# Modulation weights in runs of four row tiles, laid out by row tile

## The chip, the cores and the metric

The kernel runs on one core of one Trainium2 chip. The metric is the time of one execution on the device, in microseconds. The change was timed against the kernel before on the same chip; a profiled execution of each shows where the time goes. The core has five engines with a queue of instructions each: TensorE (PE: matmuls, PEld: its weight loads), VectorE (DVE), ScalarE (ACT), GpSimd (POOL) and SyncE (SP), which only issues transfers.

## The reference

The reference is one layer of a bidirectional encoder, applied to a prompt of 1024 tokens and a sample of 256, each with its own conditioning vector c. All is in float32 with a model width of 1024.

```python
mod = (jax.nn.silu(c) @ ada_w[l] + ada_b[l])[:, None, :]
sh1, sc1, g1, sh2, sc2, g2 = jnp.split(mod, 6, axis=-1)
h = rms_norm(x, norm_mix_g[l]) * (1 + sc1) + sh1
proj = h @ w_in[l]
...
x = x + g1 * ((g_na * y_na + g_mla * y_mla) @ w_out[l])
h2 = rms_norm(x, norm_ffn_g[l]) * (1 + sc2) + sh2
x = x + g2 * hierarchical_moe(h2, ...)
```

The modulation is a vector times a matrix of 1024 x 6144, for two vectors. Its first third (sh1, sc1) scales the input of the projections and is needed at once. The second (g1, sh2) and the third (sc2, g2) are needed only after the attention. The projection to 3,968 columns gives queries, keys and values of a neighbourhood attention, the latents of a second attention (with normalized latents and a rotary part), and the logits of the gates.

## The kernel before

The order of the work is written out by hand: each engine runs its instructions in the order of the program, and waits for other engines and for transfers by semaphores. What an operation waits for is worked out from the tiles that it reads and writes.

All large tiles are slots of one pool, 49 of 128 x 1024 floats (`Slots`, 4 KB in each partition). `get` takes the slot that has been free longest, `put` gives it back at once in program order. The next user of a slot then waits on its own engine until the last reader is through, and that can be a transfer that stores the slot to HBM.

The change lies in the stretch in which the input projections run, about 79 to 327 us of the span. The three chunks of tokens are 512, 512 and 256 wide. `work(g, ...)` does one group of 128 columns of w_in: its matmuls (line 432: each operand is split into a high and a low half, three products), then the split of the next group's weights (line 182 on ACT the high half, line 183 on DVE the low half), the load of the group after it, and the evacuation of PSUM. The groups are lat[1], qq (queries), kk (keys), gt (gates) and vv (values). The functions that `work` is given after the group run in between:

- `latent_stat` and `latent_norm` (PE line 519, DVE lines 522 and 524, ACT line 523) normalize the latents.
- `uq_part(n)` (PE line 557) projects the latents to queries. For n of 4 and 5 it is followed by `rope`, for each of the three chunks: DVE shuffles and scales (lines 536 to 538), POOL adds (line 539), then `split_out` splits the sum (ACT line 399, DVE line 400) and SP stores it (line 405, rq_d).
- `split_out` after the query and key groups does ACT line 402 or 399, DVE line 403 or 400, and stores at line 405 as well (naq_d, nak_d).
- `ukv_part` (PE line 570) and `vml_part` (PE line 584) come later.

Between all of these, `ada_step` does a little of the second and third modulation, so that it costs no stretch of its own. The weights of one row tile (128 rows of the 1024) for a half of a third of the modulation are 128 x 1024 numbers. POOL loads them (line 370); PE multiplies them in four matmuls of 32 weight columns and 256 moving columns, which stand side by side in the four quarters of the array (line 382, tile_position), and so sum up in PSUM over the eight row tiles. When a modulation is complete, DVE adds the bias (line 387) and SP stores it (line 389). There are 2 x 2 x 8 = 32 row tiles.

The order of the calls that the change moves along:

```python
work(gt[0], lambda: latent_norm(0))
work(qq[2], lambda: latent_norm(1, 2), lambda: lat_split("uq", uq_raw, 768))
work(qq[3], uq(4))
work(gt[1], uq(5))
uq_done()
work(gt[2], uq(0))
work(kk[0], uq(1))
```

Each `work` has one call of `ada_step` behind the group and one behind each function.

Of the kernel before, what the change touches and what calls it, by code (L numbers as in the profile page):

```python
# [33 lines left out]
def by_blocks(x):  # L34

    return np.ascontiguousarray(x.reshape(*x.shape[:-2], 16, 8, 8, x.shape[-1]).swapaxes(-4, -3)).reshape(x.shape)
# [54 lines left out]
def v3(t, k):  # L91
    return t.rearrange("p (k n) -> p k n", k=k)
# [3 lines left out]
def kernel(ctx, tc, A, out_p, out_s, upto=99, dbg=None):  # L96
    nc = tc.nc
    ctx.enter_context(tc.manual_schedule())
    V, S, G, PE, SY = nc.vector, nc.scalar, nc.gpsimd, nc.tensor, nc.sync
# [11 lines left out]
    def pool(name, bufs=1, space=None, stack=None):  # L111
        kw = dict(name=name, bufs=bufs, reuse_waits="tile")
        if space is not None:
            kw["space"] = space
        return (stack or ctx).enter_context(tc.tile_pool(**kw))
# [21 lines left out]
    sl = Slots(pool("slots"), NSLOT)  # L137
# [22 lines left out]
    ada_v = A["ada_w"].rearrange("o (p j) n -> (o p) j n", j=8)  # L160
# [54 lines left out]
    cT = small.tile([128, 8, 32], F32, name="cT")  # L215
# [9 lines left out]
    def bias_load(s):  # L225
        b = small.tile([128, 512], F32, name="biasz")
        G.memset(b, 0.0)
        for r in range(2):
            if s:
                SY.dma_start(b[r:128:32], A["ada_b"][:, s * 2048:(s + 1) * 2048].rearrange("o (g n) -> (o g) n", g=4))  # L230
            else:
                for v in range(2):
                    SY.dma_start(b[64 * v + r:64 * v + 64:32].rearrange("p (h n) -> p h n", h=2),
                                 A["ada_b"][:, v * 1024:(v + 1) * 1024].rearrange("o (h q n) -> (o q) h n", h=2, q=2))
        return b
# [94 lines left out]
    for j in range(KD):  # L330
# [7 lines left out]
        for n, (a, b) in enumerate(((0, hH), (1, hH), (0, hL))):  # L338
            for i in range(2):
                for c, (c0, w) in enumerate(CHUNKS):  # L340
                    PE.matmul(ps0[i][c][:, :w], order[0].at(a, j, i * 128, 128), b.at(j, c),  # L341
                              start=(j == 0 and n == 0 and (c < 2 or i == 0)), stop=(j == KD - 1 and n == 2),
                              skip_group_check=(c == 2))
    for j in range(KD):
        for c, (c0, w) in enumerate(CHUNKS):
            PE.matmul(pk[32 * c:32 * c + 32, :w], v3(kr, 8)[:, j, :32], xT.at(j, c), start=(j == 0), stop=(j == KD - 1),
                      tile_position=(0, 32 * c), skip_group_check=True)
# [11 lines left out]

    adas = [(s, hf, j) for s in (1, 2) for hf in range(2) for j in range(8)]
    ada_q = []
    ada_pm = {}

    def ada_pre():
        if adas:
            s, hf, j = adas.pop(0)
            t = sl.get()
            G.dma_start(v3(t, 4), ada_v[:, j, s * 2048:(s + 1) * 2048].rearrange("p (g n) -> p g n", g=4)[:, :, hf * 256:hf * 256 + 256])  # L370
            ada_q.append((s, hf, j, t))

    def ada_step():
        if not ada_q:
            return
        s, hf, j, t = ada_q.pop(0)
        if (hf, j) == (0, 0):
            ada_pm[s] = psm.tile([128, 512], F32, name="pm0" if s == 1 else "pmt")
            biasz[s] = bias_load(s)
        pm = ada_pm[s]  # L380
        for g in range(4):
            PE.matmul(pm[32 * g:32 * g + 32, hf * 256:hf * 256 + 256], cT[:, j, :], v3(t, 4)[:, g, :],
                      start=(j == 0), stop=(j == 7), tile_position=(0, 32 * g), skip_group_check=True)
        sl.put(t)
        if (hf, j) == (1, 7):
            row = small.tile([128, 512], F32, name="modrow")
            V.tensor_add(row, pm, biasz[s])
            for r in range(2):
                SY.dma_start(mod_d[s - 1, r].rearrange("(g n) -> g n", n=512), row[r:128:32, :])
        ada_pre()  # L390
# [17 lines left out]
    def work(g, *after):  # L408


        gi = order.index(g)
        def ahead():
            if gi + 1 < len(order):
                order[gi + 1].split()
            if gi + 2 < len(order):
                order[gi + 2].load()

        g.run(ahead)
        ada_step()
        for f in after:  # L420
            f()
            ada_step()
        g.put()
# [27 lines left out]
            sl.put(t)  # L451
        return f

    for _ in range(3):
        ada_pre()
    order[1].split()
    order[2].load()
# [544 lines left out]
            next(fill_it)  # L1002
        work(gt[i])
    while ada_q:
        ada_step()
    for x in (hH, hL):
        for c in (1, 2):
            x.put(c)
# [65 lines left out]
    n = len(units)  # L1074
# [388 lines left out]
    for c, (c0, w) in enumerate(CHUNKS):  # L1463
# [25 lines left out]
        if c == 1:  # L1489
# [3 lines left out]
            t = sl.get(ring=rows)  # L1493
# [211 lines left out]
def layout(inputs):  # L1705

    a = {k: np.ascontiguousarray(inputs[k]) for k in _INS}
    q = a["w_uq"].reshape(1, 256, 8, 96)
    a["w_uq"] = np.ascontiguousarray(np.concatenate(
        [q[..., :64].reshape(1, 256, 512), q[..., 64:].reshape(1, 256, 256)], axis=2))  # L1710
    kv = a["w_ukv"].reshape(1, 128, 8, 128)
    a["w_ukv"] = np.ascontiguousarray(np.concatenate(
        [kv[..., :64].reshape(1, 128, 512), kv[..., 64:].reshape(1, 128, 512)], axis=2))
    inv = (np.float32(1.0) / np.power(np.float32(10000.0), np.arange(0, 32, 2, dtype=np.float32) / np.float32(32)))
    ang = np.arange(SP, dtype=np.float32)[:, None] * inv[None, :].astype(np.float32)
    c, s = np.cos(ang).astype(np.float32).T, np.sin(ang).astype(np.float32).T
    cs = np.stack([np.tile(np.concatenate(x), (4, 1)) for x in ((c, c), (-s, s))])
    a["rope_p"] = by_blocks(cs[..., None])[..., 0]
    a["rope_s"] = np.ascontiguousarray(cs[:, :, :SS])
    a["x_prompt"] = by_blocks(a["x_prompt"])  # L1720

    rpb = a.pop("na_rpb")[0]
    row, c8, col = np.arange(16), np.arange(8), np.arange(64)
    rs = np.clip(row - 4, 0, 8)
    rows = (row[None, :] >= rs[:, None]) & (row[None, :] < rs[:, None] + 8)
    dr = np.clip(row[None, :] - row[:, None] + 7, 0, 14)
    dc = 8 * (np.arange(3)[None, :, None] - 1) + c8[None, None, :] - c8[:, None, None]
    val = rpb[:, dr[:, None, None, :, None], np.clip(dc + 15, 0, 30)[None, :, :, None, :]]  # L1730
    m0 = np.broadcast_to(rows[:, None, None, :, None], val.shape[1:]) & (np.abs(dc) < 16)[None, :, :, None, :]
    m1 = m0 & ((dc >= -8) & (dc < 8))[None, :, :, None, :]
    a["nbias"] = np.ascontiguousarray(np.stack(
        [np.where(m, val, np.float32(NEG)).reshape(8, 128, 384) for m in (m0, m1)], axis=2).reshape(8, 128, 768))
    st = np.clip(col - 8, 0, 48)
    inside = (col[None, :] >= st[:, None]) & (col[None, :] < st[:, None] + 16)
    dr = np.arange(6)[None, :] + 5 - np.arange(2)[:, None]
    dc = np.clip(col[None, :] - col[:, None] + 15, 0, 30)
    val = rpb[:, dr[:, None, :, None], dc[None, :, None, :]]
    a["sbias"] = np.ascontiguousarray(np.where(inside[None, None, :, None, :], val, np.float32(NEG)).reshape(8, 128, 384))  # L1740
    return a
# [18 lines left out]
```

## Time and profile before

| | |
|---|---|
| times of three runs | 1855.3, 1858.37, 1858.37 us (median 1858.37) |
| the profiled execution | 1854.83 us, of which the span of its instructions is 1853.1 |
| PE | 1743.1 us busy, 94% of the span |
| PE's weight loads | 1357.6 us, 73% |
| DVE, ACT, POOL | 1001.4, 838.8 and 319.0 us (54, 45 and 17%) |
| granted TensorE clock | 0.973 of full in the mean |
| transfers | 439.47 MB, 237 GB/s in the mean |
| modulation loads by POOL | 32 of 512 KB, in the median 6.1 us from issue to landing |

Busy time counts an engine's own instructions, not the time in which it waits; a matmul's duration overlaps that of the next one, so that the distance between two starts is its cost, not its duration. A float32 matmul stands in the trace as two records (a row tile of the modulation is eight), a matmul of the split halves as one. In the rows of waits and of the order of time, "<-" in brackets names what ended an engine's idle time.

### The profile page before, as it was taken

To read this page: it belongs to the slowest core of one execution; us is meant where nothing else is said; L and a number is where in the kernel's file an instruction comes from. 1 tells how busy PE (TensorE), PEld (TensorE's weight loads), DVE (VectorE), ACT (ScalarE), POOL (GpSimd) and SP (SyncE) were. 2 spreads that over 40 slices of the span, in tenths; PEclk is the share of its full clock that TensorE was granted. 3 is DMA by queue.
4 is the path that set the end of the run, shared out by engine and by line. 5 is a ranking of instruction groups with operands and counts; after the bars stand their busy time and mean duration, and the time that the engine had idled before them with its cause. 6 is when DMAs were issued, how large, how long until landed. Compare 5 with 4: busy or idle time off the path is not lost.

```text
span 1853.1 us, 27078 instructions
## 1 busy us (share of the span) xinstructions
PE 1743.1 (94%) x9874; PEld 1357.6 (73%) x9874; DVE 1001.4 (54%) x1674; ACT 838.8 (45%) x1391; POOL 319.0 (17%) x329
## 2 busy tenths in 40 slices
PE   5999999999999999999899999699999999999991
PEld 4787777998888888767688877567676676766760
DVE  6324422111455655444357466777777777777764
ACT  6222222321455555666533213366556565655642
POOL 0010210000122222322333000111111111111110
PEclk9989999999999999999899999799999999999995
DMA  9335676536714442878977356899999999999916
GB/s 349 109 115 168 222 264 221 191 91 165 152 55 112 115 121 86 232 214 230 297 251 224 132 216 235 327 359 360 361 365 360 362 356 361 358 356 364 349 36 242
DMA packets 268848, 439.47 MB, mean 237 GB/s; under 512 B 31928, under 2 KB 131592, under 8 KB 268712
## 3 DMA queue, kind: packets, MB, share of 16 engines
q1 hardware_dynamic: 252008, 389.45, 62.8%
q0 software_dynamic: 13824, 37.77, 7.3%
q10 hardware_dynamic: 2880, 10.49, 1.4%
q8 instruction: 79, 1.29, 0.3%
q14 instruction: 57, 0.47, 0.1%
HBM read 367.53 MB, written 82.67 MB: 243 GB/s over the span
## 4 chain that ended last, share of the span: by engine, by line
PE 84%; DVE 5%; DMA 5%; issue 2%; ACT 2%; SPq 1%; POOL 1%; DVEq 0%; POOLq 0%; ACTq 0%; another core or an unknown queue 0%
PE ph L1540 19%; PE pg L432 13%; PE py L1566 11%; PE s L895 6%; PE pw L1303 5%; PE fp L766 5%; PE fp L678 4%; PE o L945 4%; PE tp L927 4%; PE pg L599 3%; PE pt L1527 2%; PE pg L341 1%; PE pg L557 1%; PE pt L1553 1%; DMA x_d<-s,idx 1%
## 5 line engine op out<-in xcount | busy, mean ns | idle before, releaser
L1540 PE MATMUL ph<-s,s 128*128 128x512 f32 x1536 | 377.0, 401 | 1.4 <-DVE s L1530 1.2
L1399 ACT CAST s<-s 128x1024 fp32r<-128x1024 f32 x256 | 265.9, 1055 | 194.2 <-PE ph L1540 193.9
L1540 PEld LDWEIGHTS ph<-s,s 128*128 128x128 f32 x1536 | 286.4, 188 | 73.8 <-issue 13.9
L1400 DVE TENSOR_TENSOR s<-s,s 128x1024 fp32r<-128x1024 f32 x256 | 304.5, 1221 | 63.7 <-ACT s L1399 57.4
L432 PE MATMUL pg<-s,s 128*128 128x512 f32 (+1 forms) x1416 | 270.2, 351 | 7.8 <-ACT s L182 4.2
L432 PEld LDWEIGHTS pg<-s,s 128*128 128x128 f32 x1416 | 226.8, 190 | 53.0 <-ACT s L182 4.9
L1566 PE MATMUL py<-s,aT 128*128 128x512 f32 x512 | 225.1, 592 | 0.7 <-ACT aT L1555 0.7
L917 POOL TENSOR_SCALAR s<-s,m 128x1024 f32<-128x1024 f32 (+2 forms) x160 | 122.8, 767 | 438.5 <-DVE m L916 363.6
L1566 PEld LDWEIGHTS py<-s,aT 128*128 128x128 f32 x512 | 94.8, 190 | 108.2 <-issue 100.0
L895 PE MATMUL s<-s,s 96*128 96x512 f32 (+2 forms) x592 | 147.7, 368 | 1.8 <-ACT s L913 1.4
L913 ACT ACTIVATE s<-s,m 128x1024 f32<-128x1024 f32 (+2 forms) x160 | 124.9, 781 | 46.6 <-DVE m L903 27.3
L929 ACT COPY s<-tp 128x512 f32<-128x512 f32 (+2 forms) x160 | 78.2, 488 | 120.5 <-PE tp L927 116.9
L895 PEld LDWEIGHTS s<-s,s 96*128 96x128 f32 (+1 forms) x592 | 109.9, 190 | 27.9 <-ACT s L913 2.3
L678 PE MATMUL fp<-s,s 128*128 128x512 f32 x384 | 126.4, 430 | 2.8 <-ACT s L682 2.6
L927 PE MATMUL tp<-ident,s 128*128 128x128 f32 x752 | 110.4, 275 | 9.8 <-POOL s L917 9.4
L183 DVE TENSOR_TENSOR s<-s,s 128x1024 fp32r<-128x1024 f32 x31 | 37.7, 1224 | 148.7 <-ACT s L182 137.0
L1303 PE MATMUL pw<-s,s 128*128 128x512 f32 x480 | 118.0, 400 | 0.0
L766 PE MATMUL fp<-s,s 128*128 128x512 f32 (+1 forms) x576 | 114.0, 359 | 2.8 <-DMA s<-ao_m 1.4
L903 DVE TENSOR_REDUCE m<-s 128x1 f32<-128x1024 f32 (+1 forms) x80 | 85.0, 1062 | 51.6 <-PE s L895 50.2
L1572 POOL DMA_INDIRECT x_d<-s,idx x32 | 71.7, 2242 | 231.1 <-DVE s L1571 116.1
L766 PEld LDWEIGHTS fp<-s,s 128*128 128x128 f32 x576 | 96.5, 191 | 20.1 <-DMA s<-ao_m 2.1
L927 PEld LDWEIGHTS tp<-ident,s 128*128 128x128 f32 x752 | 89.3, 141 | 25.3 <-POOL s L917 15.9
(225 smaller groups left out, 2012.3 us busy)
## 6 DMA issues: line engine op xcount, KB each, us to landing
s<-in_expert_w SPq DMA_DIRECT2D x384, 512.0 KB
s<-in_w_in SPq DMA_DIRECT2D x47, 512.0 KB
s<-in_ada_w POOLq DMA_DIRECT2D x32, 512.0 KB, 6.1
s<-nak_d SPq DMA_DIRECT2D x40, 256.0 KB
s<-in_x_prompt SPq DMA_DIRECT2D x16, 512.0 KB
s<-in_ada_w SPq DMA_DIRECT2D x16, 512.0 KB
s<-gate_d SPq DMA_DIRECT2D x16, 512.0 KB
gate_d<-s SPq DMA_DIRECT2D x16, 384.0 KB
```

The costliest lines, as they stand in the source:

```text
L432: PE.matmul(p[:m, :CHUNKS[c][1]], g.at(a, j, 0, m), b.at(j, c), start=(j == 0 and n == 0), stop=(j == KD - 1 and n == 2))
L678: PE.matmul(p, w.at(a, j), b.at(j, 0), start=(n == 0), stop=(n == 23))
L766: PE.matmul(p[:, :w], b.ws[i].at(u, x * 4 + j), o[:, v, :w], start=(m == 0), stop=(m == 11))
L895: PE.matmul(u.s[:, b, :u.w], a, c, start=(n == 0), stop=(n == len(ops) - 1))
L913: S.activation(u.out, u.src, AF.Exp, bias=u.m[:, 0:1], scale=u.sign, accum_out=u.m[:, 1:2])
L917: G.tensor_scalar(u.P[:, :u.n], u.P[:, :u.n], u.m[:, 2:3], 1.0, op0=OP.mult, op1=OP.mult)
L927: PE.transpose(tp[:w, i // 128, :], u.P[:, b * 512 + i:b * 512 + i + w], ident)
L1303: PE.matmul(b.p, x[b.c].at(k, b.c, b.k), w[:, k % 2, :], start=(k + i == 0), stop=(k == 7 and i == 2))
L1399: S.copy(hi, r)
L1400: V.tensor_sub(lo, r, f32(hi))
L1540: PE.matmul(p, a[:, 2 * q + k, :], v3(w, 2)[:, k, :], start=(q + k + i == 0), stop=(q == 3 and k == 1 and i == 2))
L1566: PE.matmul(p, b.aT_[:, k, :], w[:, hb * 512:hb * 512 + 512], start=(k == 0), stop=(k == 3))
```

## The change

The second and third modulation are computed in parts of two row tiles. `ada_pre` loads the two tiles of a part, `ada_part` multiplies them and calls for the next load. `ada_step` counts its calls and does nothing in three of four; in every fourth it does two parts, that is 16 matmuls in a row. Two parts are loaded ahead at the start (four tiles) where three tiles were. The weights are put into a new order on the host, by third, half and row tile, so that a load reads 128 rows of 4 KB that follow each other, where it read four pieces of 1 KB for each of 128 rows.

```diff
--- before.py
+++ after.py
@@ -359,30 +359,38 @@
-    adas = [(s, hf, j) for s in (1, 2) for hf in range(2) for j in range(8)]
-    ada_q = []
-    ada_pm = {}
+    adas = [(s, hf, k) for s in (1, 2) for hf in range(2) for k in range(4)]
+    ada_q, ada_pm, ada_turn = [], {}, [0]
     def ada_pre():
+
         if adas:
-            s, hf, j = adas.pop(0)
-            t = sl.get()
-            G.dma_start(v3(t, 4), ada_v[:, j, s * 2048:(s + 1) * 2048].rearrange("p (g n) -> p g n", g=4)[:, :, hf * 256:hf * 256 + 256])
-            ada_q.append((s, hf, j, t))
+            s, hf, k = adas.pop(0)
+            ts = [sl.get() for _ in range(2)]
+            for i, t in enumerate(ts):
+                G.dma_start(t, A["ada_rest"][s - 1, hf, 2 * k + i])
+            ada_q.append((s, hf, k, ts))
     def ada_step():
-        if not ada_q:
-            return
-        s, hf, j, t = ada_q.pop(0)
-        if (hf, j) == (0, 0):
+
+        ada_turn[0] += 1
+        if ada_q and ada_turn[0] % 4 == 0:
+            for _ in range(2):
+                ada_part()
+
+    def ada_part():
+        s, hf, k, ts = ada_q.pop(0)
+        if (hf, k) == (0, 0):
             ada_pm[s] = psm.tile([128, 512], F32, name="pm0" if s == 1 else "pmt")
             biasz[s] = bias_load(s)
         pm = ada_pm[s]
-        for g in range(4):
-            PE.matmul(pm[32 * g:32 * g + 32, hf * 256:hf * 256 + 256], cT[:, j, :], v3(t, 4)[:, g, :],
-                      start=(j == 0), stop=(j == 7), tile_position=(0, 32 * g), skip_group_check=True)
-        sl.put(t)
-        if (hf, j) == (1, 7):
+        for i, t in enumerate(ts):
+            j = 2 * k + i
+            for g in range(4):
+                PE.matmul(pm[32 * g:32 * g + 32, hf * 256:hf * 256 + 256], cT[:, j, :], v3(t, 4)[:, g, :],
+                          start=(j == 0), stop=(j == 7), tile_position=(0, 32 * g), skip_group_check=True)
+        sl.put(*ts)
+        if (hf, k) == (1, 3):
             row = small.tile([128, 512], F32, name="modrow")
             V.tensor_add(row, pm, biasz[s])
             for r in range(2):
@@ -451,7 +459,7 @@
             sl.put(t)
         return f
-    for _ in range(3):
+    for _ in range(2):
         ada_pre()
     order[1].split()
     order[2].load()
@@ -1002,7 +1010,7 @@
             next(fill_it)
         work(gt[i])
     while ada_q:
-        ada_step()
+        ada_part()
     for x in (hH, hL):
         for c in (1, 2):
             x.put(c)
@@ -1719,6 +1727,9 @@
...
+    a["ada_rest"] = np.ascontiguousarray(
+        a["ada_w"][0, :, 2048:].reshape(128, 8, 2, 4, 2, 256).transpose(2, 4, 1, 0, 3, 5).reshape(2, 2, 8, 128, 1024))
```

The lines behind the change shift by 8 in the new file: 432 becomes 440, 557 becomes 565, 539 becomes 547, 399 becomes 407; 370 is now 371 and 382 is 390. In the order of the instructions three places change as follows.

PE at the end of group qq[3], before: the last matmuls of the group, one row tile of the modulation, and uq(4).

```order
L432 MATMUL pg<-s_598,s_1298 128x512
L432 MATMUL pg<-s_541,s_1298 128x256
L382 MATMUL pm_821<-s_1319,cT 32x256 x4
L557 MATMUL pg<-s_1199,s_1367 128x512
L557 MATMUL pg<-s_1201,s_1367 128x512
```

The same place now:

```order
L440 MATMUL pg<-s_598,s_1300 128x512
L440 MATMUL pg<-s_541,s_1300 128x256
L390 MATMUL pm_957<-s_1208,cT 32x256 x4
L390 MATMUL pm_957<-s_1209,cT 32x256 x4
L390 MATMUL pm_957<-s_1220,cT 32x256 x4
L390 MATMUL pm_957<-s_1221,cT 32x256 x4
L565 MATMUL pg<-s_1183,s_1357 128x512
L565 MATMUL pg<-s_1185,s_1357 128x512
```

Four row tiles stand where one stood; the ones that stood earlier and later in the neighbourhood, between the other groups, are gone from there.

POOL around the rotary parts, before: the modulation loads, and the additions of uq(4) (s_1487 to s_1519) and of uq(5) (s_1607 to s_1639).

```order
L370 DMA s_1319<-in_ada_w 128x4x256
L370 DMA s_1365<-in_ada_w 128x4x256
L370 DMA s_1379<-in_ada_w 128x4x256
L370 DMA s_1478<-in_ada_w 128x4x256
L539 TENSOR_TENSOR s_1487<-s_1487 128x512
L539 TENSOR_TENSOR s_1503<-s_1503 128x512
L539 TENSOR_TENSOR s_1519<-s_1519 128x256
L370 DMA s_1532<-in_ada_w 128x4x256
L370 DMA s_1598<-in_ada_w 128x4x256
L539 TENSOR_TENSOR s_1607<-s_1607 128x512
L539 TENSOR_TENSOR s_1623<-s_1623 128x512
L539 TENSOR_TENSOR s_1639<-s_1639 128x256
```

POOL now, with the additions of uq(4) from s_1489 and of uq(5) from s_1597:

```order
L371 DMA s_1466<-in_ada_rest 128x1024
L371 DMA s_1467<-in_ada_rest 128x1024
L371 DMA s_1478<-in_ada_rest 128x1024
L371 DMA s_1479<-in_ada_rest 128x1024
L547 TENSOR_TENSOR s_1489<-s_1489 128x512
L547 TENSOR_TENSOR s_1505<-s_1505 128x512
L547 TENSOR_TENSOR s_1521<-s_1521 128x256
L547 TENSOR_TENSOR s_1597<-s_1597 128x512
L547 TENSOR_TENSOR s_1613<-s_1613 128x512
L547 TENSOR_TENSOR s_1629<-s_1629 128x256
```

Four loads in a row come ahead of the additions of uq(4), and none between those of uq(4) and uq(5).

ACT at the rotary parts, before; the number after s is the slot. Lines 399 make the high half of each chunk, of uq(4) in the first three rows and of uq(5) after the gate's two.

```order
L399 CAST s38_1492<-s35_1487 128x512
L399 CAST s22_1508<-s39_1503 128x512
L399 CAST s35_1524<-s38_1519 128x256
L182 CAST s39_1584<-s41_1460 128x1024
L449 ACTIVATE s45_1590<-pg_1534 128x512
L449 ACTIVATE s45_1590<-pg_1535 128x256
L399 CAST s41_1612<-s46_1607 128x512
L399 CAST s24_1628<-s45_1623 128x512
L399 CAST s46_1644<-s41_1639 128x256
```

ACT now:

```order
L407 CAST s45_1494<-s35_1489 128x512
L407 CAST s45_1510<-s29_1505 128x512
L407 CAST s45_1526<-s35_1521 128x256
L182 CAST s29_1580<-s43_1444 128x1024
L457 ACTIVATE s17_1586<-pg_1530 128x512
L457 ACTIVATE s17_1586<-pg_1531 128x256
L407 CAST s43_1602<-s40_1597 128x512
L407 CAST s43_1618<-s17_1613 128x512
L407 CAST s43_1634<-s40_1629 128x256
```

The high halves of the three chunks went to three slots (s38, s22, s35, and then s41, s24, s46); now they go to one slot three times (s45, and then s43).

## Rows read from the trace of the kernel before

**Rows 1.** The time by stretches: length, PE busy (instructions), granted clock, DMA share, GB/s.

```profile
79.00:163.00 84.00, 84.00 (x470) 0.92 0.39 122
163.00:218.00 55.00, 51.34 (x315) 1.00 0.53 177
218.00:327.00 109.00, 109.00 (x639) 1.00 0.75 254
```

**Rows 2.** What PE waited for, 60 to 345 us: total, times, longest.

```profile
PE pg L432 <- DVE s L183: 2.5, 2, 1.5
PE pg L432 <- DVE s L522: 1.2, 1, 1.2
```

**Rows 3.** Order of time, PE, 163 to 220 us: start, us, [idle before <- releaser].

```profile
163.18 0.64 PE L382 MATMUL pm<-s,cT 128*32 128x256 f32 x8
...
165.21 1.07 PE L382 MATMUL pm<-s,cT 128*32 128x256 f32 x16
166.21 0.73 PE L432 MATMUL pg<-s,s 128*128 128x512 f32 x2
168.12 13.82 PE L432 MATMUL pg<-s,s 128*128 128x256 f32 x70 [1.18 <-DVE s L522]
181.88 0.64 PE L382 MATMUL pm<-s,cT 128*32 128x256 f32 x8
...
186.10 0.64 PE L382 MATMUL pm<-s,cT 128*32 128x256 f32 x8
186.67 8.59 PE L432 MATMUL pg<-s,s 128*128 128x512 f32 x48
195.19 0.64 PE L382 MATMUL pm<-s,cT 128*32 128x256 f32 x8
...
201.96 8.04 PE L432 MATMUL pg<-s,s 128*128 128x512 f32 x44 [1.01 <-DVE s L183]
...
217.76 2.48 PE L432 MATMUL pg<-s,s 128*128 128x512 f32 x11 [1.46 <-DVE s L183]
```

**Rows 4.** Order of time, PE, behind the last modulation matmuls.

```profile
326.44 8.59 PE L432 MATMUL pg<-s,s 128*128 128x512 f32 x48
334.87 3.59 PE L584 MATMUL pg<-s,s 128*128 128x512 f32 x15
```

**Rows 5.** Order of time, PE: the first matmul behind a run.

```profile
94.71 0.50 PE L432 MATMUL pg<-s,s 128*128 128x512 f32 x1
```

**Rows 6.** Line 432, 121 to 340 us: duration in ns, min/median/max.

```profile
L432 PE MATMUL pg<-s,s x850: 274/390/796, 121.6 to 339.9; 128*128 128x512 f32 x99, 128*128 128x256 f32 x71
```

**Rows 7.** Order of time, DVE: the normalization that PE waited for.

```profile
167.24 0.74 DVE L522 SCALAR_TENSOR_TENSOR s<-s,gq,pg 128x512 f32<-128x512 f32 x1
```

**Rows 8.** Order of time, the other engines, 182 to 202 us.

```profile
182.98 1.79 SPq L405 DMA_DIRECT2D naq_d<-s  x3
185.90 0.01 DVE L536 LOAD_MASK_SELECT s<-pg  x1 [2.03 <-DMA naq_d<-s]
...
188.06 1.28 POOL L539 TENSOR_TENSOR s<-s 128x512 f32<-128x512 f32 x1 [8.43 <-DMA naq_d<-s]
...
190.75 7.75 SPq L405 DMA_DIRECT2D rq_d<-s  x3
...
194.00 0.62 ACT L399 CAST s<-s 128x512 fp32r<-128x512 f32 x1 [4.00 <-POOL s L539]
...
197.25 0.41 ACT L399 CAST s<-s 128x256 fp32r<-128x256 f32 x1 [2.63 <-POOL s L539]
...
200.68 1.23 DVE L183 TENSOR_TENSOR s<-s,s 128x1024 fp32r<-128x1024 f32 x1 [2.56 <-DMA rq_d<-s]
```

**Rows 9.** The chain that ended last, 198 us: start, us, what.

```profile
198.14 2.34 DMA rq_d<-s
```

**Rows 10.** Line 370, loads of modulation weights: issue in ns, landing in us.

```profile
L370 POOL DMA_DIRECT2D s<-in_ada_w x29: 748/751/767, 77.6 to 296.1; - x29
...
DMA to landing us min/median/max: 4.0/5.8/9.2
```

## The prediction

> **What bounds the kernel now.** I read the busy time by stretches first: from 79 to 327 us, where the change lies, PE is busy for all of the first and the last stretch and idle for 3.7 us of 55 between 163 and 218 [rows 1]. Then the waits of PE: these 3.7 us are three waits, two for the low halves of split weights (L183) and one for the normalization of the latents (L522) [rows 2]. So PE sets the pace before 163 and after 218, but not between: there the engines behind PE do, and PE's time counts only where it ends last.
>
> **What one run of modulation matmuls costs.** A row tile is four matmuls of 256 columns on 32 weight columns each. Two starts apart give its time: alone it holds PE for 0.57 us (186.10 to 186.67), two tiles together for 1.00 (165.21 to 166.21) [rows 3]. So a tile is 0.43 us and each run pays 0.14 us once. It also costs at both edges. 48 matmuls with a run behind them take 8.52 us to the start of the run (186.67 to 195.19), with none behind 8.43 (326.44 to 334.87): 0.09 us [rows 3, 4]. The first matmul behind a run takes 0.50 us where the middle one takes 0.39: about 0.10 [rows 5, 6]. A run costs 0.33 us beside its tiles. In the order of the instructions there are 28 runs before (one of three tiles, two of two, 25 of one), now eight of four: 32 tiles both times. Were PE the end everywhere, 20 runs fewer would give 6.6 us.
>
> [...]
>
> **Part by part.** I number the calls of the step function as turns; before, each of turns 1 to 32 did a tile, now turns 4, 8, ... 32 do four.
>
> Stretch 1, to the end of qq[2] at 163.18: before six runs with eight tiles, now two runs with eight. PE has no wait there, so 4 x 0.33 = 1.3 us are gained.
>
> Stretch 2, from 163.18 to the end of qq[3] at 181.88. Turns 9, 10 and 11 ran here beside the chain ACT, DVE (L403, L522), which starts from the end of qq[2]. PE nonetheless waited 1.18 us, until 168.12, for the L522 that ends at 167.98 [rows 3, 7]. Taking 3 tiles away from PE ahead of that wait only makes the wait longer, by 1.3 us and two runs: nothing gained. What is late next is the same L522.
>
> Stretch 3, from 181.88 to 217.76. Here qq[3]'s three stores, the rotary parts of uq(4) and uq(5) and their stores form one chain over DVE, POOL, ACT and DMA, and PE waits twice for its ends, at 201.96 and 217.76 [rows 3, 8]. Before, turns 12 to 17 lay under it; now turns 12 and 16 with four tiles each do (they are 2 x (4 x 0.43 + 0.33) = 4.1 us of PE, no more than the six runs, 6 x 0.76 = 4.6, so PE is not late). The change makes this chain longer in three places.
> - POOL. Turn 12 now queues four loads ahead of uq(4)'s first addition (L539). The buffers of the first three were last read by qq[3]'s three stores, issued between 182.98 and 184.77; the first landed at about 185.9, 2.9 us after its issue (DVE waited for it), a half-sized one 2.3 us after its issue [rows 8, 9]. So the third load can start at 187.1 to 187.7, and third and fourth take 0.75 us each on POOL [rows 10]: the addition starts at 188.6 to 189.2 instead of 188.06. I take +1.0, by the row of POOL's own DMAs. The upper end is 1.5, if each store lands half a microsecond later. The lower end is -0.6: DVE's 2.03 us of waiting for the first store go, since that buffer now comes from the modulation, and uq(4) starts four tiles instead of one into the turn, 1.3 us later; were the loads no hindrance at all, the difference would be the gain. Behind the addition wait ACT (L399), DVE (L400) and the store.
> - ACT, uq(4). All three chunks now write their split halves into one buffer. The second waits for the first one's store: issued at 190.75, it lands by 193.7 if it takes 2.9 us, and ACT came at 194.00 anyway: no cost. The third waits for the second's: that was issued about 1.4 us after ACT's copy of 194.00 (as 190.75 stands to the copy behind the addition of 188.06 to 189.34), at 195.4, and lands at 197.7 to 198.3, where ACT started at 197.25 [rows 8, 9]. +0.4 to +1.1, taken as 0.9, the full-sized store's.
> - ACT, uq(5): the same once more, +0.9. Its first load wait is gone (turns 13 to 15 issue nothing now), which takes nothing off: POOL's additions waited for DVE.
>
> Then the last store lands, L183 makes the low half of the next weights, and PE goes on: +2.8 us (ends 0.2 and 3.7) against the end of qq[3].
>
> [...] No row shows a POOL load of long pieces, so the sum goes by the 0.75 us.
>
> Stretch 4, from 217.76 to turn 32: before 14 runs with 15 tiles (turns 18 to 32), now 4 runs with 16. PE has no wait there before; DVE, ACT and the weight loads are ready early. 10 x 0.33 - 0.43 = 2.9 us gained. If the waits came back here, they would take this.
>
> The layout itself I cost at nothing: the loads are 0.5 MB each as before and land 4 to 9 us after their issue [rows 10], and with four turns between, each has over 20 us. The early load that is added at the start (four tiles instead of three) shares the bandwidth with modulation 0's weights; if it made their matmuls late, that would be 1 to 2 us, an estimate from the 4.0 us in which a lone load lands. The granted clock is below full for a part of the first stretch (0.92 in the mean [rows 1]); the matmuls around which it falls stay where they are, and I count no change.
>
> **Sum.** -1.3 + 0 + 2.8 - 2.9 = -1.4 us. The profiled execution took 1854.83 (span 1853.1, 1.7 around it), so it would take 1853.4. The median of the runs shown is 1858.37, 3.5 above it; the same step from there is 1857.0, which I predict. The bounds give -4.0 to -0.5.
>
> **Rivals.**
>
> - PE is the end everywhere, 1851.8 (-6.6). For it: 99% busy over the three stretches [rows 1]. Against: the wait at 168.12 and those at 201.96 and 217.76 stand right behind turns that go, and the ends of these waits come from other engines [rows 2, 3].
> - The buffers run short, slower: 1861.9. The four loads move 2 MB while uq(4)'s stores go out. A load lands in 4.0 us alone, 5.8 in the middle of the others [rows 10]; a store stretched the same way takes 2.9 x 5.8 / 4.0 = 4.2 us instead of 2.9. It decides from 3.25 us on, the distance from the first chunk's store to the second's copy (190.75 to 194.00) [rows 8]; beyond it every chunk waits for the store ahead. 1.0 us for uq(4)'s second chunk, 1.3 for its third and for its last store, and 1.3 for the last of uq(5), beside turn 16's loads: 4.9 on top of -1.4 is +3.5. Against: the loads are issued by about 189 and the first store a microsecond after, so that most of the 2 MB is through by then.
>
> **Chances.** My sum with its bounds 0.66, PE everywhere 0.18, buffers short 0.16. Two measurements of this kernel agree within about 0.2%, 3.7 us, and below that nothing can be told. Faster by more: the first rival and the low end of the sum, 0.28. Slower by more: about half of the second rival, and what I have not seen, 0.12. Within: 0.60. The range, 1851.5 to 1861.5, takes in the first rival and all of the second but its end; the sum's own range is 1854.4 to 1857.9.
>
> **What would show it.** PE's runs of the modulation line: 8, each about 1.9 us from its start to the next matmul. Stretch 1 about 1.3 us shorter; from the end of qq[2] to the end of qq[3] 18.7 us as before, with a wait of 2.5 to 3 us for L522's successor. POOL's four loads between qq[3]'s stores and the first addition. In stretch 3, from the end of qq[3] to the second wait for split weights, 37 to 39.5 us instead of 35.9, the two waits together 4 us or more. From there to the last turn no wait, and 2.9 us less. I am wrong if the waits for split weights do not grow, if PE waits in the last stretch, or if the matmuls in a run of four take more than 0.43 us a tile.

## The result, and the profile after

The changed kernel takes 1866.76 us in the median of six runs (1860.46 to 1869.32), the kernel before 1855.53 (six runs): a ratio of 1.0054, 95% interval 1.0035 to 1.0073. It is slower by about 10 us, and lies outside the range that was forecast (1851.5 to 1861.5). The forecast started from the median of the first three runs of the kernel before, 1858.37, which the six runs put 2.8 lower: it expected -1.4 us, and about +10 was measured. The profiled execution took 1864.43 us with a span of 1862.7, 9.6 more than that of before.

By stretches, bounded by the same places as in the forecast (end of qq[2]; second wait for the low half of split weights; end of turn 32). This is the view of [rows 1] for the kernel after: stretch, length, PE busy (instructions), the other engines, granted clock, DMA share, GB/s.

```profile
79.00:161.58 82.58, 82.58 (x476) 69.22 (x471) 20.23 (x37) 17.88 (x33) 8.06 (x12) 0.94 0.36 118
161.58:226.15 64.57, 52.02 (x306) 41.40 (x304) 28.22 (x54) 14.80 (x27) 10.76 (x14) 0.95 0.54 181
226.15:333.84 107.69, 107.69 (x644) 88.78 (x644) 30.16 (x45) 28.32 (x51) 6.84 (x13) 0.98 0.70 239
```

The middle stretch was 54.58 us (163.18 to 217.76 in [rows 3]) and is 64.57: the loss is there. 12.5 us of the longer stretch are waits of PE, where 3.7 were [rows 2]. At the end of turn 32 the kernel after is 7.4 us late (333.84 against 326.44 in [rows 4]); the other 2.2 us of the span come behind that, where nothing was changed, and their cause stays open. The waits of PE of the kernel after, 60 to 345 us:

```profile
PE pg L440 <- DVE s L183: 6.3, 2, 4.6
PE pg L440 <- ACT s L182: 3.8, 1, 3.8
PE pg L440 <- DVE s L530: 2.3, 1, 2.3
PE pg L440 <- DVE s L411: 0.2, 1, 0.2
```

A wait for the high half (L182) was not there before, nor the small one for L411. The waits for the low half (L183) have grown from 2.5 to 6.3 us, and that for the normalization (L522 before, L530 now) from 1.2 to 2.3. PE in the order of time, the places of [rows 3]:

```profile
166.51 13.84 PE L440 MATMUL pg<-s,s 128*128 128x256 f32 x70 [2.29 <-DVE s L530]
180.28 1.93 PE L390 MATMUL pm<-s,cT 128*32 128x256 f32 x32
182.15 3.73 PE L565 MATMUL pg<-s,s 128*128 128x512 f32 x18
...
201.64 1.64 PE L440 MATMUL pg<-s,s 128*128 128x512 f32 x4 [3.82 <-ACT s L182]
204.96 9.88 PE L440 MATMUL pg<-s,s 128*128 128x512 f32 x44 [1.68 <-DVE s L183]
...
226.15 10.21 PE L440 MATMUL pg<-s,s 128*128 128x512 f32 x43 [4.60 <-DVE s L183]
```

A run of four tiles holds PE for 1.87 us (180.28 to 182.15), as forecast. The end of qq[3] is 1.60 us earlier than before (181.88), the second wait for the low half ends 8.39 later (217.76). The other engines between the two, the places of [rows 8]:

```profile
181.39 2.84 SPq L413 DMA_DIRECT2D naq_d<-s  x3
...
185.07 0.68 DVE L546 SCALAR_TENSOR_TENSOR s<-s,s 128x512 f32<-128x512 f32 x1
186.00 0.53 POOL L371 DMA_DIRECT2D s<-in_ada_rest  x1 [40.91 <-DVE s L546]
187.27 1.73 POOL L371 DMA_DIRECT2D s<-in_ada_rest  x3 [0.74 <-DMA naq_d<-s]
189.06 1.29 POOL L547 TENSOR_TENSOR s<-s 128x512 f32<-128x512 f32 x1
...
196.06 0.62 ACT L407 CAST s<-s 128x512 fp32r<-128x512 f32 x1 [5.06 <-DMA rq_d<-s]
...
200.23 0.41 ACT L407 CAST s<-s 128x256 fp32r<-128x256 f32 x1 [3.55 <-DMA rq_d<-s]
...
215.90 2.13 POOL L371 DMA_DIRECT2D s<-in_ada_rest  x4
216.92 0.41 ACT L407 CAST s<-s 128x256 fp32r<-128x256 f32 x1 [3.57 <-DMA rq_d<-s]
...
224.87 1.23 DVE L183 TENSOR_TENSOR s<-s,s 128x1024 fp32r<-128x1024 f32 x1 [7.09 <-DMA rq_d<-s]
```

POOL's loads stand between DVE's last step (until 185.75) and the addition (189.06). ACT waits three times for a store of the chunk ahead (the buffer is the same), and DVE at the end 7.09 us for the last store of uq(5). The chain that ended last shows how long these stores took:

```profile
191.75 4.23 DMA rq_d<-s
...
214.10 2.74 DMA rq_d<-s
...
217.81 6.94 DMA rq_d<-s
```

The third one is of a quarter of a megabyte and took 6.94 us, where a store of that size took 2.34 in [rows 9]. The transfers between 217.8 and 222.0 us, by queue (packets, MB, share of the 16 engines):

```profile
q0 software_dynamic: 385, 1.43, 99.3%
```

That is POOL's queue alone (from 212 to 228 us it moved 2.10 MB, which are the four loads). SP's queue, in which the store had been since 217.81, moved nothing in these 4.2 us, while the four loads that POOL issued from 215.90 on were being served. Then both queues are served side by side. The same view from 222.0 to 224.8 us, in which SP's part also holds some of the load of weights that SP issued behind the store (at 218.26):

```profile
q1 hardware_dynamic: 759, 0.51, 56.1%
q0 software_dynamic: 162, 0.54, 48.6%
```

So the store first moved nothing for 4.2 us, and then shared the engines with what was left of the loads. Why it moved nothing up to 222.0 us (385 packets of the one queue, none of the other), no run here shows.

### The profile page after: what moved, and what is told of

The parts are those of the page before. It is cut to its first block, busy times and chain, and to the rows that moved or that the text cites. A ratio compares the mean times of both kernels' runs of the same rounds, so it can differ in the third digit from the quotient of the medians.

```text
span 1862.7 us, 27085 instructions
## 1 busy us (share of the span) xinstructions
PE 1740.3 (93%) x9874; PEld 1361.0 (73%) x9874; DVE 1001.2 (54%) x1674; ACT 838.2 (45%) x1391; POOL 311.9 (17%) x329
## 4 chain that ended last, share of the span: by engine, by line
PE 75%; DMA 5%; DVE 4%; issue 2%; ACT 2%; POOL 1%; SPq 0%; DVEq 0%; POOLq 0%; ACTq 0%; another core or an unknown queue 0%
PE ph L1548 19%; PE py L1574 11%; PE pg L440 8%; PE s L903 6%; PE pw L1311 5%; PE fp L774 5%; PE fp L686 4%; PE o L953 4%; PE tp L935 4%; PE pg L607 3%; PE pt L1535 2%; DMA s<-in_w_in 1%; DMA rq_d<-s 1%; PE pt L1561 1%; DMA x_d<-s,idx 1%
## 5 line engine op out<-in xcount | busy, mean ns | idle before, releaser
L440 PE MATMUL pg<-s,s 128*128 128x512 f32 (+1 forms) x1416 | 274.6, 355 | 16.4 <-ACT s L182 7.7
L440 PEld LDWEIGHTS pg<-s,s 128*128 128x128 f32 x1416 | 230.9, 193 | 58.8 <-ACT s L182 8.2
L183 DVE TENSOR_TENSOR s<-s,s 128x1024 fp32r<-128x1024 f32 x31 | 37.7, 1223 | 149.8 <-ACT s L182 133.7
```

The source lines that it names most:

```text
L440: PE.matmul(p[:m, :CHUNKS[c][1]], g.at(a, j, 0, m), b.at(j, c), start=(j == 0 and n == 0), stop=(j == KD - 1 and n == 2))
```

## The experiments

Theory A: what costs are loads in bursts, because stores issued behind them are held up by them. Theory C: what costs is that slots are short, because a slot handed on at once puts the landing of a store on the chain. Rivals: B, the layout; and that long runs on PE cost by themselves (two of the expectations call this one rival C; it is not theory C). Each kernel was timed against the kernel before on the same chip, but not all on one chip: the kernel before took 1855.5 us where the first four were timed, 1854.9 for the next four and 1855.1 for the last three. Differences between two experiments are differences of medians, and where the chips differ these 0.7 us are in them. The diffs are shortened at "...", with comments added.

### The layout alone

```diff
-            G.dma_start(v3(t, 4), ada_v[...])
+            G.dma_start(t, A["ada_rest"][s - 1, hf, j])   # one tile per turn, 3 ahead, as before
```

> Only the new layout of the weights: one row tile in every turn, three tiles loaded ahead and one load per turn as before, each load 128 rows of 4 KB. Theory A (what costs the changed kernel its time are four loads in a burst in front of the stores of the rotary parts, which are then served behind them; the layout itself is innocent): as before, within 0.2% of 1855.5, POOL's issue of a load 0.53 us instead of 0.75 (as in the changed kernel's trace). Rival B (the long rows of the new layout take the DMA engines away from the stores): slower by 4 us or more, with a store of rq_d that takes over 4 us in the chain.

1857.49 us, ratio 1.0014 (1.0006 to 1.0023): not innocent, but small, and not by rival B's way. In the profiled execution POOL issues faster (two loads in 1.09 us, 0.75 each before), and that turns two transfers around. In order of time:

```profile
198.53 1.09 POOL L371 DMA_DIRECT2D s<-in_ada_rest  x2 [1.45 <-ACT s L182]
...
199.26 0.39 SPq L455 DMA_DIRECT2D gate_d<-s  x1
...
207.95 0.01 DVE L541 LOAD_MASK_SELECT s<-pg  x1 [1.69 <-DMA gate_d<-s]
...
219.41 15.22 PE L437 MATMUL pg<-s,s 128*128 128x512 f32 x66 [1.37 <-DVE s L183]
```

The second load leaves at 199.07, 0.2 us ahead of the gate's store. In the kernel before the store came first (199.40, the load 199.43). Now it lands behind the load, and the slot that it holds, which uq(5) gets next, comes 1.7 us late. PE starts the 66 matmuls behind the second wait for the low half at 219.41, 1.65 us later than before (217.76), and runs them with a granted clock of 0.85 in 15.2 us instead of 13.1. That the turned order is the cause is read from these two profiles, and was not tested.

### Runs of four, loads one per turn

```diff
+    use = {4: 4, 8: 4, ..., 32: 4}     # tiles multiplied in a turn
+    load = {1: 1, 2: 1, ..., 32: 1}    # tiles loaded in a turn; 3 ahead
```

> Runs of four tiles on PE in turns 4, 8, ... 32 as in the changed kernel, but the loads one per turn and three ahead at the start, as before. Theory A: the first addition of uq(4) is no longer behind four loads, and no store of rq_d lies behind more than one load: the distance from the end of qq[3] to the second wait for the low half of split weights returns from 45.9 us to 36 or 37 (35.9 before), and of the saving by fewer runs -1.3 and -2.5 us (the stretches before qq[2]'s end and behind that wait) stay: 1850 to 1854, that is 1 to 5 us under the kernel before. Rival C (long runs on PE, by the pause that they make for the projections, are what costs): the time stays near 1866.

1866.79 us, ratio 1.0063 (1.0050 to 1.0076). A miss for theory A as it was put: with one load per turn the loss is the same. But up to six tiles are held until a run uses them, where four are held in the changed kernel and three before. Waits of ACT and DVE in this kernel, 182 to 232 us, and PE's, 160 to 345:

```profile
ACT s L404 <- DMA gate_d<-s: 7.3, 1, 7.3
DVE s L541 <- DMA rq_d<-s: 5.8, 2, 2.9
```

```profile
PE pg L437 <- ACT s L182: 11.4, 2, 5.8
PE pg L437 <- DVE s L527: 2.3, 1, 2.3
PE pg L437 <- DVE s L183: 1.5, 1, 1.5
```

Now the second and the third chunk of uq(5) wait 2.9 us each for the store of the chunk ahead, and the first one 7.3 us for the store of the gates, whose slot it gets; in the kernel before these waits do not exist. That is theory C, which was tested next. It is no clean test of A, though: the gates' store (issued at 208.63, 7.21 us in the chain) stands behind two loads that POOL issued from 207.92 on.

### Turn 16's loads behind the last store

```diff
-                G.dma_start(t, A["ada_rest"][s - 1, hf, 2 * k + i])
+                (SY if ada_turn[0] == 16 else G).dma_start(t, A["ada_rest"][s - 1, hf, 2 * k + i])
```

> The changed kernel, but the four loads of turn 16 are issued by SP, where they stand behind the three stores of uq(5), instead of by POOL, which issued them 0.3 to 1.9 us ahead of the last of these stores. Theory A (a store is served behind all that was issued ahead of it): the last store of rq_d takes 2.3 to 2.9 us instead of 6.9, the second wait for the low half shrinks by about 4.3 us, and the 3.4 us of half clock behind it go, which gave 1.7: 6 us under the changed kernel, about 1861. Rival (transfers share the engines, the store is long for another reason): no change to within 1.5 us.

1859.28 us, ratio 1.0021 (1.0011 to 1.0031): 7.5 us less than the changed kernel, where 6 were expected. The chain shows the last store:

```profile
221.58 2.30 DMA rq_d<-s
```

2.30 instead of 6.94 us. The same four loads are made into the same slots; what changed is the queue, and with it that they are issued behind the store (from 223.27 on).

### Turn 12's loads off POOL, but still ahead of the stores

The same line with `ada_turn[0] == 12`.

> The changed kernel, but the four loads of turn 12 are issued by SP instead of POOL: they stand ahead of uq(4)'s stores as before, but POOL's additions are no longer queued behind them. This tells POOL's queue from the traffic. By the queue alone, the first addition starts at about 185.8 us instead of 189.1 and the whole chain is 3.3 us earlier. By the traffic alone (theory A), the first store of uq(4) is issued earlier but lands only when the 2 MB ahead of it are through, at about 194 instead of 196.0, and the chain gains 2 us at most. No gain at all: ACT or DVE set the pace.

1866.27 us, ratio 1.0064 (1.0049 to 1.0078): no gain. In order of time:

```profile
188.74 1.28 POOL L547 TENSOR_TENSOR s<-s 128x512 f32<-128x512 f32 x1 [42.29 <-PE pg L565]
...
199.19 0.62 ACT L407 CAST s<-s 128x512 fp32r<-128x512 f32 x1 [8.53 <-DMA rq_d<-s]
```

uq(4) started at 184.99 here, so the first addition follows it by 3.75 us; in the changed kernel it was 6.91 (182.15 to 189.06). Waiting in POOL's queue did cost 3.2 us. But the store of the first chunk, now behind the same loads, lands only at 199.1, and ACT waits for it: the gain is given back at the next place, and the chain is not shorter.

### One more buffer for the changed kernel

```diff
+        t = extra.tile([128, 1024], F32R, name="extra") if own else sl.get(F32R)
-        split_out(t, m, c, dst, row0, p0=p0)
+        split_out(t, m, c, dst, row0, p0=p0, own=(m == 128 and c == 1))
```

> The changed kernel with one more buffer of 4 KB per partition, which takes the split halves of the middle chunk of uq(4) and uq(5), so that no chunk's copy waits for the store of the chunk ahead. Theory C (too few free slots put the landing of the stores on the chain): the waits of ACT for rq_d (12.2 us in three) go, the chain to the last store of uq(5) is 1.1 + 0.95 + 0.95 = 3.0 us shorter, and the time falls by 2.5 to 3.5 us, to about 1864; the last store stays at 7 us, since POOL's four loads still come ahead of it. If only the loads count (theory A alone): no change.

1858.02 us, ratio 1.0015 (1.0003 to 1.0028): 8.7 us less than the changed kernel (8.1 when each is taken against the kernel before on its own chip), and far more than the 3 expected. ACT's waits, 182 to 226 us, have no row for rq_d any more:

```profile
ACT s L408 <- POOL s L549: 20.1, 4, 8.8
ACT extra L408 <- POOL s L549: 8.0, 2, 4.0
ACT s L411 <- issue: 5.9, 1, 5.9
ACT s L411 <- PE pg L442: 5.8, 1, 5.8
```

From the start of uq(4) to the second low half the profiled chain takes 38.7 us (184.72 to 223.39), 42.7 in the changed kernel (182.15 to 224.87), though the last store is still behind the loads (217.59 to 223.26). The second wait for the low half is 1.6 us instead of 4.6, and no lower clock shows behind it: the 37 matmuls there took 7.51 us, 0.20 each, as the 66 before did (13.16 us). That the median fell by twice as much would fit the clock, of which more below; how much of it is the clock's is not shown.

### One slot less for the kernel before

```diff
+    held = sl.get()        # behind gt[0]
...
+    sl.put(held)           # behind uq(5)
```

> The kernel before with one slot of the pool withheld from behind gt[0] to the end of uq(5): nothing else is touched, runs of one tile, one load per turn. The three chunks of uq(4) and of uq(5) then share one slot for their split halves, as in the changed kernel. Theory C: the waits for the store of the chunk ahead appear (ACT waiting for rq_d), the chain grows by 2 to 6 us, the two waits for the low half with it, and the time is 1858 to 1862. If slots don't matter: 1855.5.

1868.43 us, ratio 1.0069 (1.0055 to 1.0082), where 1858 to 1862 were expected: 13 us from one slot of 49, more than the whole change costs, with runs of one tile, the old layout and one load per turn. Waits of all engines, 182 to 230 us:

```profile
PE pg L432 <- ACT s L182: 14.2, 2, 7.6
...
ACT s L182 <- DMA rq_d<-s: 12.5, 2, 6.3
ACT s L399 <- DMA rq_d<-s: 7.1, 2, 3.6
```

The chunks wait for the store ahead, as expected (L399). The larger wait was not foreseen: with one slot less, the high half of the next weights (L182) gets the slot of the last chunk, and waits for its store. POOL's loads stand ahead of that store here too, which takes 5.70 us in the chain, so that a part of the 13 us is theory A's.

### Runs of four only where PE sets the pace

```diff
+    use = {4: 4, 8: 4, 9: 1, ..., 17: 1, 21: 4, 25: 4, 29: 4, 32: 3}
+    load = {1: 1, 2: 1, ..., 29: 1}    # old layout, 3 ahead
```

> The kernel before (old layout, three loaded ahead, one load per turn) with runs of four only where PE sets the pace: turns 4, 8, and 21, 25, 29 (and three tiles in turn 32); turns 9 to 17 do one tile each as before. Theory: the gain by fewer runs is real where PE has no wait (-1.3 us ahead of qq[2]'s end, -2.5 to -3 behind the second wait for the low half), and everything that cost the changed kernel (longer waits, half clock behind them, few slots, loads ahead of stores) is in turns 9 to 17: 1851 to 1852.5. Rival C (long runs cost by themselves): 1856 or more.

1851.05 us, ratio 0.9983 (0.9974 to 0.9992): 3.8 us under the kernel before, as expected. Its stretches:

```profile
161.91:216.74 54.83, 50.81 (x314) 39.30 (x313) 28.30 (x54) 16.02 (x30) 11.89 (x13) 1.00 0.54 178
216.74:322.29 105.55, 105.55 (x636) 87.23 (x636) 29.71 (x45) 27.17 (x48) 10.18 (x14) 1.00 0.77 260
```

The middle is as before (54.58), and the last stretch takes 105.55 instead of 108.68 us (217.76 to 326.44) for the same 15 tiles in 4 runs instead of 14: 0.31 us for each run saved. So long runs cost nothing by themselves where PE sets the pace.

### Runs of four at other turns

```diff
-        if ada_q and ada_turn[0] % 4 == 0:
+        if ada_q and ada_turn[0] in (4, 8, 11, 14, 20, 24, 28, 32):
```

> The changed kernel with the runs of turns 12 and 16 in turns 11 and 14: turn 11 is right ahead of the wait for the normalization (2.3 us in the changed kernel), and its loads are issued a group earlier, ahead of qq[3]'s end; those of turn 14 come between uq(4) and uq(5). Theory: the wait at 168 us shrinks to about 0.5 us and no half clock follows it; the first addition of uq(4) is not behind loads, so the chain is about 3 us earlier; the last store of uq(5) is free of loads ahead of it (2.5 instead of 7 us). What stays is the one slot for three chunks (2 to 3 us) and the 1.2 us at the start: 1856 to 1860. If place doesn't matter: 1866.

1856.68 us, ratio 1.0012 (1.0001 to 1.0024): 10 us less than the changed kernel, by the place of the runs and of their loads alone. The wait ahead of qq[3] is 0.8 us, with no lower clock behind it (the 70 matmuls of qq[3] took 13.84 us, as in the changed kernel). A wait for the high half stays:

```profile
PE pg L440 <- ACT s L182: 4.3, 2, 4.0
PE pg L440 <- DVE s L183: 2.8, 2, 2.2
PE pg L440 <- DVE s L530: 0.8, 1, 0.8
```

### The hybrid with the extra buffer

```diff
+        own = c == 0 and ((dst is naq_d and row0 == 384) or (dst is rq_d and row0 == 128))
```

> The hybrid (runs of four only where PE sets the pace) with one more buffer of 4 KB per partition, for the split halves of the first chunk of qq[3] and of uq(5). In the hybrid DVE's first shuffle of uq(4) still waits for the store of qq[3]'s first chunk, because it gets the same slot (2.03 us in the kernel before). With one slot more in the rotation this wait goes and the chain over uq(4) and uq(5) starts 2 us earlier. Theory C: the two waits for the low half of split weights (1.3 and 1.6 us in the hybrid) go, but no more than these 2.9 us can be gained: 1848 to 1849.5. If slots are no longer what is short: 1851.

1849.6 us, ratio 0.9964 (0.9950 to 0.9977), 5.5 us under the kernel before and the fastest of all, though just above the range expected. One of the two waits for the low half is gone:

```profile
PE pg L441 <- DVE s L184: 1.4, 1, 1.4
PE pg L441 <- DVE s L531: 1.1, 1, 1.1
```

Its interval overlaps the hybrid's, so that the buffer's own share (about 1.5 us) is not shown.

### Two combinations

The extra buffer with the runs in turns 11 and 14, and with turn 16's loads on SP:

> Runs of four everywhere, placed as in the run with turns 11 and 14, with the extra buffer for the middle chunk's split halves of uq(4) and uq(5). Theory C: ACT's waits for rq_d at the last chunks go (1.2 and 1.0 us); with a shorter wait at the second low half the half clock behind it goes too in part: 1852.5 to 1855 (1856.7 without the buffer). If the place of the loads was all: no change.

> The changed kernel with both costs taken back at once: the extra buffer for the middle chunk's split halves, and turn 16's loads issued by SP behind uq(5)'s last store. If the two costs are separate, the last store falls from 5.8 us to 2.5 on top of the buffer's gain: 1858.0 - 3.3 = 1854.7 (1853.5 to 1856), and what is left against the hybrid (1851) is the longer wait ahead of qq[3] with the half clock behind it and the loads ahead of uq(4). If they are one and the same cost: 1858.

The first takes 1854.31 us, ratio 0.9995 (0.9986 to 1.0004), the second 1856.35, ratio 1.0005 (0.9996 to 1.0014). The first is as expected, though a new wait of 4.7 us for the low half came up: a load issued at 195.94 stood ahead of the last store of uq(4) at 196.77. The second is just above its range (1853.5 to 1856). Its gain over the extra buffer alone, 1.7 us, is not clear of noise, as the intervals overlap. By the medians the two costs are not simply added: undone alone they gave 7.5 and 8.1 us, each against the kernel before on the same chip, and together about 10; with these intervals that is hardly clear of noise. With both undone the changed kernel is level with the one before.

### The clock behind a wait

Behind the longer waits the rows show a lower granted clock. The same 70 matmuls of qq[3] behind the same wait of 2.3 us, in the run with turn 12's loads on SP and in the one with paced loads:

```profile
167.93 15.27 PE L440 MATMUL pg<-s,s 128*128 128x256 f32 x70 [2.27 <-DVE s L530]
```

```profile
167.09 16.62 PE L437 MATMUL pg<-s,s 128*128 128x256 f32 x70 [2.28 <-DVE s L527]
```

In the changed kernel's profile they took 13.84. The granted clock of these stretches is 0.89, 0.81 and 1.00. So the 2.3 us wait is followed by a lower clock in some executions and not in others, with 0, 1.4 or 2.8 us of loss. The changed kernel's profile has the half clock behind the later waits: 0.50 granted from 202.3 to 209.0 and from 226.15 to 229.55 us, and 1.00 behind each, from 209.2 to 214.76 and from 229.55 to 240.67. Of the 66 matmuls behind the last wait the longest took 0.79 us, where their median is 0.39. The stretches from the end of the high-half wait and of the second low-half wait:

```profile
201.64:214.76 13.12, 11.44 (x48) 9.09 (x49) 6.94 (x15) 1.95 (x4) 2.56 (x2) 0.74 0.42 131
226.15:240.67 14.52, 14.52 (x66) 12.25 (x67) 3.49 (x5) 2.56 (x5) 0.53 (x1) 0.88 0.43 140
```

The second has the same 66 matmuls as before had from 217.76 to 230.84: 14.52 us instead of 13.08. Of the six runs of the changed kernel the three with the lowest mean clock (0.966 to 0.967) took 1866.7 to 1869.3 us, the two with the highest (0.972) 1860.5 and 1864.4.

## Why the prediction was wrong

- **Runs on PE: right.** 0.33 us a run were taken, 0.31 measured in the hybrid. The last stretch gave 1.0 us instead of 2.9; 1.4 of the 1.9 that are missing went to the half clock at its start.
- **Stretch 1: right in sign.** Its end came 1.6 us earlier (1.3 forecast). More of it ran at full clock (0.94 in the mean, 0.92 before), and the start was 1.2 us later; the hybrid, with three early loads, had such a later start as well, and the run with turns 11 and 14, with four, had not, so that the fourth early load is not its cause. That 1.6 came so near to 1.3 is partly luck, since the start and the clock, which pull against each other, were not in the sum.
- **Stretch 2: right in the profile, wrong in general.** From the end of qq[2] to that of qq[3] it took 18.70 us both times, with a wait of 2.3 us. That a lower clock can follow a longer wait was not in the sum; it cost 1.4 to 2.8 us in the profiles of the other kernels with that wait.
- **Stretch 3: this step failed.** +2.8 us were forecast, with ends 0.2 and 3.7; against the end of qq[3] it is 8.39 + 1.60 = +10.0. By its terms: the first addition comes at 189.06, 1.0 later as forecast, but qq[3] had ended 1.6 earlier, so that against its end the term measures +2.6 (the forecast let the loads wait for qq[3]'s stores; these left 1.6 us earlier, from 181.39 instead of 182.98, and yet the second load waited for one until 187.27); uq(4)'s second chunk +1.1 where the sum took 0, since the first store took 4.23 us and not 2.9; its third chunk and uq(5)'s +0.95 each, 0.9 forecast. And the largest, which has no term in the sum at all: the last store of uq(5), behind turn 16's four loads, +4.6 (together 10.2; 0.2 came back between). The sum weighed the loads of turn 12 and the time of their issue, and not which transfer stands ahead of which one at turn 16; only the second rival put a price on that, 1.3 us. With turn 16's loads behind the store it took 2.30 us again, and the kernel 7.5 us less.
- **The second rival was what happened**, with a chance of 0.16 and too small a price. It stretched every store in proportion, to 4.2 us. For uq(4)'s first store that came out (4.23), for the last of uq(5) it did not: that one stood still for 4.2 us before its first packet moved, and took 6.94. Its point of decision, 3.25 us, was right for uq(4).
- **The issue of a load: shorter than in the sum, with little effect.** The sum went by 0.75 us, as no row showed a load of long pieces; with the new layout it took 0.53. The addition came 1.0 us later all the same, as POOL waited for slots until 187.27: the three loads behind that wait took 1.73 us, which at 0.75 each would be 2.25. By itself the layout cost 2 us.
- **What stays open.** Why the costs that were undone one by one do not add up in medians is not shown, and why the clock falls behind the same wait in some executions and not in others, no run here tells.

## What to carry to other kernels

In a pool of buffers that is nearly empty, ask of each longer hold whose buffer comes next, and whether its last reader is a store: one slot of 49 was worth 13 us here. A store on a chain was held up here by loads issued ahead of it on another queue (6.94 us instead of 2.30), so put prefetches behind the stores that someone waits for, or early. Merge small work into long runs where its engine has no wait; where it was filling waits, small pieces were the faster here (1851.05 us with long runs only outside the waits, 1866.76 with them everywhere).

## What was not expected of the hardware

A store of SP that was issued 0.3 us behind four loads of POOL got none of the DMA engines for 4.2 us, in which POOL's queue had 99.3% of them, and shared them after that. A faster issue (0.53 instead of 0.75 us) went with 2 us more for the kernel with the layout alone, where a load now stands ahead of a store. And the wait of PE of 2.3 us was followed by a lower granted clock with paced loads (0.81) and with turn 12's loads on SP (0.89), at a cost of 2.8 and 1.4 us on top of it; behind the waits of 3.8 and 4.6 us of the changed kernel stood 0.50 for 6.7 and 3.4 us. Single waits of 1.0 to 1.6 us were followed by none in the kernel before and in the two hybrids (the 70 matmuls of qq[3] took 13.82 to 13.84 us, the 66 behind the second low half 13.16); in the kernel with the layout alone two of 1.6 and 1.4, close together, were (0.85).
